# A gap of 64 bytes in SBUF: weights and the tiles they are multiplied with, moved apart modulo 128 bytes

## The chip, the core and the metric

The kernel runs on one core of one Trainium2 chip. A core has five engines that run side by side: TensorE (PE in the profile; its weight loads are shown apart as PEld), VectorE (DVE), ScalarE (ACT), GpSimd (POOL) and SyncE (SP, which here only issues DMAs). They work on tiles in SBUF, a memory of 128 partitions. A tile has the same byte offset in every partition, and this offset is what the change is about. TensorE writes its results to eight banks in PSUM.

The metric is the device time of one execution in microseconds (us). Three runs of the kernel before gave 505.38, 505.47 and 506.69 us, median 505.47 us.

## What is computed

One decoder block over 512 tokens of 1,024 channels, in float32: a norm, one wide projection, sparse attention (mixer A), chunked retention (mixer B), a gated merge, an output projection, a second norm and the residual. Cut to the lines that make the matrix products:

```python
h = rms_norm(x, norm_pre)
proj = h @ w_in
...
o_a = jax.vmap(nsa_fn)(q_n, k_c, v_c, k_s, v_s, k_w, v_w, gate_n)
y_a = (o_a * jax.nn.silu(z_n)) @ w_nsa_o
...
o_b = jax.vmap(retention_sequence)(q_r, k_r, v_r)
y_b = (o_b * jax.nn.silu(z_r)) @ w_ret_o
merged = jax.nn.sigmoid(m_a) * y_a + jax.nn.sigmoid(m_b) * y_b
x = x + rms_norm(merged @ w_out, norm_post)
```

## The kernel before

**Products in three parts.** A float32 operand is split in a high part, rounded to the type fp32r, and a low part, the rest. A product a*b is then three matmuls of fp32r that add up in one PSUM bank: high*high, low*high and high*low (`mm3`, and the same three by hand in `tra`, `seven`, `pair` and `out_seven`). In the profile the parts are named apart: `hTh` and `hTl` are the high and low parts of the transposed h, `whi` and `wlo` those of a piece of weights.

**Two ways round.** A matmul row reads `bank<-moving,stationary`: the second tile is loaded into the array (the LDWEIGHTS rows of PEld), the first one is streamed through it. `nat` streams weights against a stationary piece of h (`bank<-whi,hTh`, 512 columns). `tra` keeps a piece of weights stationary and streams h (`bank<-hTh,whi`, 512 columns). In `seven`, four quarters of a weight block and sums of them are multiplied 256 columns at a time with quarters of h (`bank<-hTh,whi`, 256 columns) and with sums of quarters of h, which lie in other tiles, named `shorts` (`bank<-shorts,whi`, 256 columns). Attention and retention multiply tiles of one large tile, `arena_r`, with each other (`bank<-arena_r`). Transpositions (L263) stream an identity matrix, `identr`, against a stationary `shorts` tile. Nearly all matmuls are issued by the helper at L257; L1234 and L1725 are the blocks `pair` and `out_seven`.

**Weights.** A stream of weights comes from DRAM by DMA into four `raw` tiles. ScalarE (L224, sometimes VectorE, L232) writes the high part to one of nine `whi` tiles, VectorE (L236) the low part to one of nine `wlo` tiles. GpSimd queues DMAs that add blocks of weights in DRAM (`pair`, `t`, `out`).

**Order.** The order of all instructions is fixed when the program is built, by a planner with costs for each engine; each engine runs its own list and waits on semaphores. The planner's costs know shapes, not addresses.

**Where tiles lie.** Pools take SBUF from low to high in the order in which they are opened: first a block `room` of 58 KB, over which tiles named `words` and `shorts` are laid, then the pools `small`, `const`, `wts` (9 `whi` and 9 `wlo`, 2,048 bytes each), `hT`, `big` (`arena_r` and `rsrow`) and `raw`. The places follow from this and from the sizes of the tiles:

| tiles | first byte, before | modulo 128, before |
|---|---|---|
| `room` (`words`, `shorts`) | 2,176 | 0 |
| `identr` | 63,104 | 0 |
| `kc`, `vcs` (compressed keys and values) | 67,488 and 68,000 | 32 |
| `whi`, `wlo` | 69,056 | 64 |
| `hTh`, `hTl` | 105,920 and 122,304 | 64 |
| `arena_r` | 138,688 | 64 |
| `raw` | 212,416 | 64 |

Almost every tile cut from these starts a multiple of 128 bytes further on, so that it keeps its class modulo 128. The exception is the second block of weights, pieces of 280 columns (1,120 bytes) in `arena_r`, whose classes go round 64, 32, 0, 96.

Of the kernel before, what the change touches and what calls it, by code (L numbers as in the profile page):

```python
# [10 lines left out]
FT = mybir.dt.float32  # L11
# [7 lines left out]
P = 128  # L19
# [131 lines left out]
def block_kernel(ctx: ExitStack, tc, x, xT, x0s, ws, small, w2s, norm_post, rope_r, dmask, out):  # L151
# [22 lines left out]
    hp_ = ctx.enter_context(tc.tile_pool(name="hT", bufs=1))  # L174
# [109 lines left out]
    nhalf = cp.tile([P, 4], FT, name="nhalf")  # L284
    G.memset(nhalf, -0.5)

    hTh = hp_.tile([P, KD, SEQ], FR, name="hTh")
    hTl = hp_.tile([P, KD, SEQ], FR, name="hTl")

# [1696 lines left out]
```

## Time and profile before

| | us |
|---|---|
| median of three runs | 505.47 |
| the profiled execution, whole | 504.99 |
| its span, first to last instruction | 503.2 |
| PE busy / PEld / DVE / ACT / POOL | 493.7 / 421.4 / 424.6 / 324.7 / 39.3 |

The profile comes from one execution. The span is what its rows add up to; 1.8 us lie around it. In a row such as `x48 | 13.6, 282` stand the number of instructions, the time in which at least one of them ran, and the mean length of one in ns. A matmul's length is longer than its share of the engine, since the next one starts before it ends: how fast TensorE goes is read from the starts of successive rows, or from a number of matmuls in a stretch without idle time.

### The profile page before, as it was taken

How to read it: one execution, taken by the hardware profiler on the slowest of the kernel's cores; microseconds unless marked ns; L12 is line 12 of the kernel's file. 1: busy time of each engine (PE TensorE's matmuls, PEld its weight loads, DVE VectorE, ACT ScalarE, POOL GpSimd, SP SyncE). 2: the span in 40 equal slices, each digit the busy share in tenths (PEclk: the TensorE clock that was granted, in tenths of full speed). 3: DMA queues.
4: the chain of work that ended last, by engine and by line, in shares of the span. 5: the costliest groups of instructions: out<-in, count | busy, mean ns of one | idle time of the engine just before them, and what ended most of it. 6: DMA issues, size and time to landing. Idle time of an engine off the chain costs nothing.

```text
span 503.2 us, 7872 instructions
## 1 busy us (share of the span) xinstructions
PE 493.7 (98%) x2666; PEld 421.4 (84%) x2666; DVE 424.6 (84%) x996; ACT 324.7 (65%) x722; POOL 39.3 (8%) x66
## 2 busy tenths in 40 slices
PE   8999999999999999999999999999999999999994
PEld 7898887888888888888888888888888989988883
DVE  6698899989989989998789999778787867979795
ACT  6795599558679788784587574835435535527642
POOL 3102100023000210000100000101000000000010
PEclk9999999999999999999999999999999999999999
DMA  8968995779998899325556673530473735635813
GB/s 318 385 211 283 326 227 200 242 136 225 370 238 182 262 293 211 113 85 166 119 173 212 215 235 114 126 126 8 162 250 113 233 116 191 199 113 169 303 56 142
DMA packets 31080, 98.75 MB, mean 196 GB/s; under 512 B 3136, under 2 KB 6976, under 8 KB 30272
## 3 DMA queue, kind: packets, MB, share of 16 engines
q1 hardware_dynamic: 24576, 70.85, 41.5%
q0 software_dynamic: 6320, 27.26, 22.9%
q8 instruction: 21, 0.34, 0.3%
q14 instruction: 19, 0.16, 0.1%
q10 hardware_dynamic: 144, 0.14, 0.1%
HBM read 93.52 MB, written 31.98 MB: 249 GB/s over the span
## 4 chain that ended last, share of the span: by engine, by line
PE 89%; DMA 5%; DVE 4%; issue 1%; ACT 0%; POOLq 0%; DVEq 0%; POOL 0%; ACTq 0%; SPq 0%
PE bank L257 70%; PE bank L1234 8%; PE bank L1725 7%; PE bank L263 4%; DMA raw<-in_stream_dram 3%; DVE arena_r L236 1%; DMA words<-in_xT_dram 1%; DVE wlo L236 1%; DMA words<-in_x_dram 1%; DVE words L236 1%; DVE words L679 0%; DVE words L249 0%; DVE words L243 0%; DVE words L967 0%; DVE whi L232 0%
## 5 line engine op out<-in xcount | busy, mean ns | idle before, releaser
L224 ACT ACTIVATE whi<-raw 128x512 fp32r<-128x512 f32 x177 | 107.0, 627 | 53.4 <-PE bank L257 36.2
L236 DVE TENSOR_TENSOR wlo<-raw,whi 128x512 fp32r<-128x512 f32 x188 | 123.4, 685 | 10.4 <-ACT whi L224 9.5
L257 PE MATMUL bank<-whi,hTh 128*128 128x512 f32 x192 | 74.0, 407 | 0.3 <-ACT hTh L224 0.3
L257 PE MATMUL bank<-arena_r 128*128 128x256 f32 (+2 forms) x328 | 70.7, 335 | 0.7 <-DVE arena_r L236 0.5
L257 PE MATMUL bank<-whi,hTl 128*128 128x512 f32 x192 | 71.2, 391 | 0.0
L257 PE MATMUL bank<-wlo,hTh 128*128 128x512 f32 x192 | 71.0, 390 | 0.0
L224 ACT ACTIVATE arena_r<-bank 128x512 fp32r<-128x512 f32 (+3 forms) x104 | 49.1, 476 | 26.3 <-PE bank L263 25.4
L236 DVE TENSOR_TENSOR arena_r<-bank,arena_r 128x512 fp32r<-128x512 f32 (+3 forms) x104 | 56.0, 542 | 9.6 <-ACT arena_r L224 8.5
L257 PE MATMUL bank<-arena_r,whi 128*128 128x512 f32 (+1 forms) x208 | 63.6, 381 | 0.0
L224 ACT ACTIVATE words<-words,stat 128x128 f32<-128x128 f32 (+3 forms) x105 | 54.1, 546 | 6.6 <-DVE stat L967 4.9
L257 PEld LDWEIGHTS bank<-arena_r 128*128 128x128 f32 x328 | 50.8, 189 | 7.6 <-DVE arena_r L236 1.2
L257 PE MATMUL bank<-hTh,whi 128*128 128x512 f32 (+1 forms) x144 | 52.2, 363 | 0.0
L257 PE MATMUL bank<-hTh,wlo 128*128 128x512 f32 (+1 forms) x144 | 51.4, 357 | 0.0
L257 PE MATMUL bank<-hTl,whi 128*128 128x512 f32 (+1 forms) x144 | 51.1, 355 | 0.0
L257 PEld LDWEIGHTS bank<-arena_r,whi 128*128 128x128 f32 x208 | 38.8, 188 | 7.3
L257 PEld LDWEIGHTS bank<-whi,hTl 128*128 128x128 f32 x192 | 36.2, 188 | 8.0
L257 PEld LDWEIGHTS bank<-whi,hTh 128*128 128x128 f32 x192 | 36.5, 191 | 6.9 <-ACT hTh L224 0.6
L257 PEld LDWEIGHTS bank<-wlo,hTh 128*128 128x128 f32 x192 | 36.1, 188 | 6.3
L257 PE MATMUL bank<-arena_r,wlo 128*128 128x512 f32 x96 | 37.3, 389 | 0.0
L263 PEld LDWEIGHTS bank<-identr,shorts 128*128 128x128 f32 x268 | 30.1, 140 | 8.6 <-DVE arena_r L236 0.9
L224 ACT ACTIVATE words<-words 128x512 f32<-128x512 f32 (+3 forms) x47 | 27.2, 586 | 12.8 <-DVE words L236 8.0
L263 PE MATMUL bank<-identr,shorts 128*128 128x128 f32 x268 | 31.6, 238 | 0.5 <-DVE arena_r L236 0.5
(182 smaller groups left out, 891.0 us busy)
## 6 DMA issues: line engine op xcount, KB each, us to landing
raw<-in_stream_dram SPq DMA_DIRECT2D x73, 512.0 KB, 4.4
pair<-in_stream_dram POOLq DMA_DIRECT2D x6, 1024.0 KB, 11.8
t<-in_stream_dram POOLq DMA_DIRECT2D x6, 1024.0 KB, 17.2
out<-in_stream_dram POOLq DMA_DIRECT2D x6, 1024.0 KB, 17.1
words<-in_x_dram SPq DMA_DIRECT2D x8, 512.0 KB, 6.9
raw<-s SPq DMA_DIRECT2D x8, 512.0 KB, 4.2
raw<-pair SPq DMA_DIRECT2D x8, 512.0 KB, 4.2
raw<-t SPq DMA_DIRECT2D x8, 512.0 KB, 3.6
```

The lines of the kernel that those rows point to most:

```text
L224: S.activation(o, i, func, **kw)
L236: (V if e == "dve" else G).tensor_tensor(o, a, b, op=op)
L257: T.matmul(ps, a, b, start=start, stop=stop)
L263: T.transpose(ps, a, idn)
L1234: T.matmul(ps[m], a, b, start=n in first and s + j == 0, stop=n in last and s + j == 5, skip_group_check=True)
L1725: T.matmul(ps[m], a, b, start=n in first and s + i == 0, stop=n in last and s + i == 5, skip_group_check=True)
```

## The change

One tile of 16 float32 (64 bytes in each partition) is taken from the pool `hT` ahead of `hTh` and is never used:

```diff
     nhalf = cp.tile([P, 4], FT, name="nhalf")
     G.memset(nhalf, -0.5)

+    hp_.tile([P, 16], FT, name="room16")
     hTh = hp_.tile([P, KD, SEQ], FR, name="hTh")
     hTl = hp_.tile([P, KD, SEQ], FR, name="hTl")
```

Every tile from `hTh` on moves up by 64 bytes; `room`, `identr`, `kc`, `vcs`, `whi` and `wlo` stay where they are. Each engine has the same instructions in the same order as before, PE 2,653 matmuls among them; only addresses differ.

| a matmul's moving and stationary tile | modulo 128, before | after |
|---|---|---|
| weights with `hTh`, `hTl` or `arena_r`, either way round | 64 and 64 | 64 and 0, or 0 and 64 |
| `arena_r` with `arena_r` or `hTh` | the same class (or 280-column pieces, all four differences) | the same differences |
| `shorts` with weights | 0 and 64 | 0 and 64 |
| `identr` with `shorts` | 0 and 0 | 0 and 0 |
| VectorE's low part: `raw`, `whi` read, `wlo` written | 64, 64, 64 | 0, 64, 64 |

The four `raw` tiles, 192 past a multiple of 256 bytes before, come to multiples of 256.

## The prediction

> **What bounds the kernel now.** I read the page first, then the windows, then the chain of waits.
>
> ```profile
> span 503.2 us, 7872 instructions
> ...
> PE 493.7 (98%) x2666; PEld 421.4 (84%) x2666; DVE 424.6 (84%) x996; ACT 324.7 (65%) x722; POOL 39.3 (8%) x66
> ...
> PE 89%; DMA 5%; DVE 4%; issue 1%; ACT 0%; POOLq 0%; DVEq 0%; POOL 0%; ACTq 0%; SPq 0%
> ```
>
> TensorE is busy 493.7 of 503.2 us and is 89% of the chain that ended last. The windows (PE, PEld, DVE, ACT, POOL busy with counts, granted clock, DMA share, GB/s) show where that is strict:
>
> ```profile
> 34.00:100.00 66.00, 64.58 (x378) 54.78 (x377) 60.64 (x159) 50.27 (x116) 6.34 (x10) 1.00 0.81 251
> 100.00:250.00 150.00, 150.00 (x804) 125.98 (x804) 133.15 (x373) 110.39 (x291) 18.11 (x22) 1.00 0.77 199
> 250.00:355.00 105.00, 105.00 (x543) 88.93 (x542) 91.41 (x197) 69.17 (x135) 6.37 (x8) 1.00 0.50 154
> 355.00:495.00 140.00, 140.00 (x782) 122.65 (x782) 110.42 (x196) 68.42 (x128) 1.69 (x2) 1.00 0.52 173
> ```
>
> From 100 to 495 us TensorE has no idle time at all, at a granted clock of 1.00. A nanosecond less per matmul is there a nanosecond less in the end, as long as VectorE, at 133 of 150 us the next, keeps up. So the question is only the step from one matmul to the next. The chain, in order of time (start, length, what), gives the step of the wide ones:
>
> ```profile
> 354.67 103.93 PE bank L257 x621
> 458.59 35.37 PE bank L1725 x156
> ```
>
> The 156 matmuls of 512 columns at L1725 take 35.37 us: 226.7 ns each, with both tiles 64 past a multiple of 128. Now the narrow ones, 256 columns, in `seven` (timeline: start, length):
>
> ```profile
> 391.10 0.28 PE L257 MATMUL bank<-hTh,wlo 128*128 128x256 f32 x1
> ...
> 392.18 0.28 PE L257 MATMUL bank<-hTh,wlo 128*128 128x256 f32 x1
> ...
> 392.66 0.39 PE L257 MATMUL bank<-shorts,whi 128*128 128x256 f32 x2
> ...
> 393.68 0.39 PE L257 MATMUL bank<-shorts,whi 128*128 128x256 f32 x2
> ```
>
> From the first to the second row nine matmuls start in 1.08 us, 120 ns each; from the third to the fourth nine in 1.02 us, 113.3 ns each. Shape, stationary weights, loop and clock are the same. What differs is where the moving tile lies: `hTh` at 64, in the class of the weights, `shorts` at 0, in the other. And 113.3 is exactly half of 226.7: both are the step in which the columns alone set the pace, and `hTh` pays 6.7 ns on top. I read this as two streams of one engine, the moving columns and the next weight load, that get in each other's way when they lie in the same half of 128 bytes; that a 512-column matmul pays nothing in a steady run means that its longer step hides the collision. After the change every such pair of weights with `hTh`, `hTl` or `arena_r` stands as `shorts` with weights stands now.
>
> **The change, term by term.** No instruction is added, removed or moved on any queue, and no wait. Only steps can change.
>
> Narrow matmuls with h moving and weights stationary, and the same with `shorts`, grouped by form:
>
> ```profile
> L257 PE MATMUL bank<-shorts,whi 128*128 128x256 f32 x112 | 21.0, 277 | 0.0
> L257 PE MATMUL bank<-shorts,wlo 128*128 128x256 f32 x64 | 17.7, 277 | 0.0
> L257 PE MATMUL bank<-hTh,wlo 128*128 128x256 f32 x48 | 13.6, 283 | 0.0
> L257 PE MATMUL bank<-hTl,whi 128*128 128x256 f32 x48 | 13.6, 282 | 0.0
> L257 PE MATMUL bank<-hTh,whi 128*128 128x256 f32 x48 | 13.6, 282 | 0.0
> L257 PE MATMUL bank<-arena_r,whi 128*128 128x256 f32 x16 | 4.5, 281 | 0.0
> ```
>
> 3 x 48 + 16 = 160 matmuls change class, all between 385 and 437 us, where nothing but TensorE decides: 160 x 6.7 ns = **1.07 us less**. The bounds are nothing (the class isn't the cause) and the same 1.07 us.
>
> Wide matmuls in the mixed stages. The lengths of one, from the forms between 40 and 350 us, and two rows from 350 to 497 us:
>
> ```profile
> L257 PE MATMUL bank<-whi,hTh 128*128 128x512 f32 x160 | 64.5, 403 | 0.0
> L257 PE MATMUL bank<-whi,hTl 128*128 128x512 f32 x160 | 62.6, 391 | 0.0
> L257 PE MATMUL bank<-wlo,hTh 128*128 128x512 f32 x160 | 62.5, 390 | 0.0
> L257 PE MATMUL bank<-hTh,whi 128*128 128x512 f32 x91 | 36.7, 404 | 0.0
> L257 PE MATMUL bank<-hTh,wlo 128*128 128x512 f32 x91 | 35.8, 394 | 0.0
> L257 PE MATMUL bank<-hTl,whi 128*128 128x512 f32 x91 | 35.6, 391 | 0.0
> ...
> L257 PE MATMUL bank<-arena_r,whi 128*128 128x512 f32 x192 | 59.2, 389 | 0.0
> L257 PE MATMUL bank<-arena_r,wlo 128*128 128x512 f32 x96 | 37.3, 389 | 0.0
> ```
>
> In the steady stage one lasts 389 ns. In the mixed stages the four kinds that don't come first behind a transposition last 1 to 5 ns more, and the step is longer by as much, as the timeline shows:
>
> ```profile
> 166.04 0.46 PE L257 MATMUL bank<-whi,hTh 128*128 128x512 f32 x1
> 166.34 0.39 PE L257 MATMUL bank<-wlo,hTh 128*128 128x512 f32 x1
> ...
> 168.43 0.39 PE L257 MATMUL bank<-whi,hTl 128*128 128x512 f32 x1
> ```
>
> From 166.34 to 168.43 nine wide matmuls start, 232 ns each in place of 226.7: a matmul that has been put off by short ones before it makes up for it only over many steps, as one would expect where a wide one has no slack. The sum over the four rows is 160 x 2 + 160 x 1 + 91 x 5 + 91 x 2 = 1,117 ns for 502 matmuls, 2.2 ns each; the same 2.2 ns for the 251 of the two first kinds (whose means of 403 and 404 hold a pause of some 75 ns behind a transposition, 166.04 to 166.34, that is no matter of addresses) make 0.56 us more. Bounds: nothing, and 1.7 us. With the other class there is slack to catch up, but the short matmuls before (arena with arena, transpositions) still collide, since their classes don't change. I take half: **0.85 us less**.
>
> Narrow matmuls of the hidden layer (`bank<-whi,arena_r`, about 75 to 97 us) change class too, but there TensorE waits for the low part:
>
> ```profile
> 76.16 0.38 PE L257 MATMUL bank<-wlo,arena_r 128*128 128x256 f32 x1 [0.47 <-DVE wlo L236]
> ...
> L263 PE MATMUL bank<-identr,shorts 128*128 128x128 f32 x268 | 31.6, 238 | 0.5 <-DVE arena_r L236 0.5
> ```
>
> 64 of them x 6.7 ns would be 0.43 us; what hides it is that wait, which grows by what the matmuls save. I count nothing.
>
> Pairs that get worse: the 268 transpositions stand in some 67 groups of four. Behind a group, `identr` moves at 0 while a piece of h or arena is loaded, at 64 before and at 0 after; ahead of it, an h or arena tile moves at 0 while `shorts` is loaded. At most 67 x 2 x 6.7 ns = 0.9 us more; the pause of 75 ns behind each group and the wide matmul ahead of it should cover most. I take **0.15 us more**, bounds 0 and 0.9.
>
> VectorE and ScalarE read `raw` at 0 in place of 64. VectorE's subtraction with tiles at 0 and 64 read and 64 written is there already, from `words`:
>
> ```profile
> L236 DVE TENSOR_TENSOR wlo<-raw,whi 128x512 fp32r<-128x512 f32 x188 | 123.4, 685 | 10.4 <-ACT whi L224 9.5 <-PE bank L257 0.4
> L236 DVE TENSOR_TENSOR arena_r<-words,arena_r 128x512 fp32r<-128x512 f32 x15 | 10.1, 682 | 0.0
> ```
>
> 682 against 685 ns: 3 ns x 188 = 0.6 us of VectorE at most, off the chain. Nothing. DMAs into `raw` are on the chain only in the first 26 us, in two pieces:
>
> ```profile
> 9.66 7.84 DMA raw<-in_stream_dram
> ...
> 18.77 6.68 DMA raw<-in_stream_dram
> ```
>
> [...]
>
> **Sum.** 1.07 + 0.85 - 0.15 = 1.77 us less: 504.99 becomes 503.22 us. The profiled execution is 0.48 us below the median of the runs, so a median of **503.7 us**.
>
> **Rivals.**
>
> *Nothing happens.* What sets `shorts` apart may be another thing than bit 6 of the address: `shorts` lie in the first 62 KB, all else behind. For it: only one pair of tiles shows the gain. Against it: weights with h and arena with weights lie in quite different places and all stand at 120 or 226.7. Time 505.4. [...]
>
> *Only the narrow ones gain.* The wide ones' 2.2 ns come from something else in the mixed stages, and the loss at the transpositions is somewhat larger: between 0.5 and 1.5 us less, at the middle 504.5.
>
> *Slower: the wide ones lose.* If the collision hangs on where in the step the weight load reads, the wide ones may be free of it now because of the equal class, and pay with unequal ones. For it: the one place where a wide matmul at 64 is followed by a load from 0 is the one ahead of a transposition, and it is slow:
>
> ```profile
> 208.82 0.40 PE L257 MATMUL bank<-whi,hTl 128*128 128x512 f32 x1
> 209.06 0.45 PE L263 MATMUL bank<-identr,shorts 128*128 128x128 f32 x4
> ```
>
> 0.24 us in place of 0.227. Against it: a transposition is another kind of load, and narrow ones are free with unequal classes. Price 6.7 ns for each of the 753 + 288 wide matmuls of the rows above, 7.0 us, less the 1.07 of the narrow ones: 505.5 + 5.9 = 511.4. It decides as soon as more than 1.77 us / 6.7 ns = 264 wide matmuls pay.
>
> **Chances and range.** The forecast, with all between 1.5 and 3.2 us less (1.07 + 1.7 + 0.43): 0.52. Only the narrow ones: 0.19. Nothing, within 0.5 us: 0.21. Slower: 0.08. A measurement of this kernel tells about 0.3%, 1.5 us, from no change. Faster by more than that: 0.52; within: 0.40; slower: 0.08. The range goes from 505.5 - 3.2 = 502.3 to 505.8, nothing gained and a third of the 0.9 us lost at transpositions; the slower rival is left out.
>
> **What would show it.** Right: narrow `hTh,whi` at 113 ns a step and a length of 277; the four wide kinds at 389 to 390 in the mixed stages; 156 matmuls at L1725 in 35.4 us as before. Wrong: `hTh,whi` still at 120 (then it is not the class), L1725 at 36.4 us (then wide ones pay), or new waits of TensorE for `wlo` between 100 and 250 us (then VectorE takes the gain).

## The result, and the profile after

| | median, us | lowest to highest | profiled execution, us | its span, us |
|---|---|---|---|---|
| before | 505.50 | 505.38 to 506.69 (4 runs) | 504.99 | 503.2 |
| after | 509.91 | 509.25 to 510.25 (4 runs) | 509.25 | 507.5 |

The ratio is 1.008, with a 95% interval from 1.0061 to 1.010: the kernel is 4.4 us slower, where 1.8 us less was forecast. The page of the kernel after (span, busy time of the engines, shares of the chain that ended last):

```profile
span 507.5 us, 7872 instructions
...
PE 498.2 (98%) x2666; PEld 421.2 (83%) x2666; DVE 424.8 (84%) x996; ACT 325.2 (64%) x722; POOL 39.2 (8%) x66
...
PE 95%; DVE 2%; issue 1%; DMA 1%; ACT 0%; POOLq 0%; POOL 0%; DVEq 0%; ACTq 0%
```

TensorE is busy for 4.5 us more (498.2 against 493.7) with the same number of instructions (2,666 matmul rows in both pages; the 2,653 given with the change stands in neither), VectorE and ScalarE for 0.2 and 0.5 us more. So no wait has come in: the same matmuls take longer. TensorE's share of the chain, 95% against 89%, is no part of the loss: before, the chain ran over DMAs up to 25.45 us, here it runs over TensorE from 4.65 us on, and the 121st matmul starts 28.7 us into the span before and 28.8 after. The windows (busy time with counts of PE, PEld, DVE, ACT, POOL, then granted clock, DMA share, GB/s) say the same by stage:

```profile
34.00:100.00 66.00, 64.56 (x378) 54.74 (x377) 60.99 (x161) 50.73 (x116) 6.30 (x10) 1.00 0.82 251
100.00:250.00 150.00, 150.00 (x795) 124.75 (x795) 131.60 (x367) 109.99 (x289) 18.11 (x22) 1.00 0.76 198
250.00:355.00 105.00, 105.00 (x535) 87.65 (x535) 89.97 (x196) 67.17 (x131) 6.37 (x8) 1.00 0.49 149
355.00:495.00 140.00, 140.00 (x777) 121.53 (x777) 110.27 (x194) 68.82 (x127) 1.69 (x2) 1.00 0.51 170
```

From 100 to 495 us TensorE still has no idle time and the granted clock is still 1.00, but in the same three stretches it gets 9, 8 and 5 matmuls less done (804, 543 and 782 before). The end of the chain, in order of time (start, length, what):

```profile
357.35 104.67 PE bank L257 x621
462.03 36.20 PE bank L1726 x156
```

(Lines behind the new one are numbered one higher: L1726 is L1725 of before.) Against the rows of before, 354.67 with 103.93 and 458.59 with 35.37, the stages up to the last transposition bring 357.35 - 354.67 = 2.68 us, the 621 matmuls behind it 0.74 us, the last 156 another 0.83 us: together 4.25 of the span's 4.3. These 156 wide matmuls go at 36.20 / 156 = 232.1 ns a step in place of 226.7. Lengths, by form, between 40 and 350 us:

```profile
L257 PE MATMUL bank<-whi,hTl 128*128 128x512 f32 x160 | 63.2, 395 | 0.0
L257 PE MATMUL bank<-wlo,hTh 128*128 128x512 f32 x160 | 63.1, 394 | 0.0
...
L257 PE MATMUL bank<-hTl,whi 128*128 128x512 f32 x88 | 34.6, 394 | 0.0
L257 PE MATMUL bank<-hTh,wlo 128*128 128x512 f32 x88 | 34.6, 393 | 0.0
```

and between 350 and 501 us:

```profile
L257 PE MATMUL bank<-arena_r,whi 128*128 128x512 f32 x192 | 59.6, 392 | 0.0
...
L257 PE MATMUL bank<-shorts,wlo 128*128 128x256 f32 x64 | 18.0, 281 | 0.0
L257 PE MATMUL bank<-hTh,wlo 128*128 128x256 f32 x48 | 13.4, 278 | 0.0
...
L1726 PE MATMUL bank<-whi,arena_r 128*128 128x512 f32 x32 | 10.1, 396 | 0.0
```

Apart from those that come first behind a transposition, wide matmuls with weights moving are longer in every row, 394 to 396 ns (389 to 391 before); those with weights stationary last 392 to 394 (389 to 394 before), longer in all rows but `hTh` over `wlo`, 393 against 394. Narrow ones with h fell from 283 to 278, near the 277 of the forecast, but those with `shorts`, which like the weights did not move at all, rose from 277 to 281. From the starts of successive rows, summed over the whole trace (what a start comes later than 226.7 or 113.3 ns behind the one before, longer pauses left out): wide with weights moving 0.94 to 5.24 us, wide with weights stationary 0.62 to 1.56, narrow with h 1.01 to 0.52, narrow with `shorts` 0.16 to 0.77. Those four bring 5.4 us; all other steps, the longer pauses of TensorE among them, give 1.1 back.

### The profile page after: what moved, and what is told of

Same layout as the page of the kernel before. It is cut to its first block, busy times and chain, and to the rows that moved or that the text cites. A ratio compares the mean times of both kernels' runs of the same rounds, so it can differ in the third digit from the quotient of the medians.

```text
span 507.5 us, 7872 instructions
## 1 busy us (share of the span) xinstructions
PE 498.2 (98%) x2666; PEld 421.2 (83%) x2666; DVE 424.8 (84%) x996; ACT 325.2 (64%) x722; POOL 39.2 (8%) x66
## 4 chain that ended last, share of the span: by engine, by line
PE 95%; DVE 2%; issue 1%; DMA 1%; ACT 0%; POOLq 0%; POOL 0%; DVEq 0%; ACTq 0%
PE bank L257 76%; PE bank L1235 8%; PE bank L1726 7%; PE bank L263 4%; DVE arena_r L236 1%; DMA words<-in_x_dram 1%; DVE wlo L236 1%; DVE words L249 0%; DVE words L236 0%; DVE words L968 0%; DVE words L243 0%; ACT words L224 0%; POOLq L1983 0%; POOL rr L236 0%; DVEq L1983 0%
```

## The experiments

The theories that the expectations name by letters: **A**, the prediction's own rule turned round, only bit 6 of the difference counts and unequal halves cost the wide matmuls time; **B**, h and `arena_r` at multiples of 128 are bad in themselves; **C**, it is `raw` at multiples of 128 or 256; **D**, any move costs, by higher bits of the address; **E**, what counts is the stationary tile's address less the moving one's, modulo 256 or 512, and 0 is the one place that is free for wide matmuls; **F**, the two places don't matter, another engine's traffic does; **G**, narrow matmuls have two lasting states, and what runs ahead of them decides which. In E, weights moving over h (`nat`) and h moving over weights (`tra`) have opposite differences: with a gap of 64, `nat` stands at 64 and `tra` at 192. The diffs are against the kernel after; ratios are against runs of the kernel before on the same chip, whose medians were 505.53 (e1 to e4), 505.73 (e5 to e8) and 505.13 (e9 to e11).

**A gap of 128.** Weights, h and `arena_r` are all 64 past a multiple of 128 again, at a difference of 128.

```diff
-    hp_.tile([P, 16], FT, name="room16")
+    hp_.tile([P, 32], FT, name="room16")
```

> The gap is 128 bytes in place of 64: h, arena and raw are back at 64 past a multiple of 128, at other addresses than before. Theory A (a matmul's step depends on the difference modulo 128 bytes between its moving tile and the stationary tile loaded beside it; wide matmuls, 512 columns, pay for unequal halves of 128): 505.5 us, the 156 matmuls at the out block in 35.4 us. Theory B (h and arena at multiples of 128 are bad in themselves): 505.5 us. Theory C (raw at multiples of 128 or 256 is bad for those who read or write it): 505.5 us. Theory D (any move of these tiles makes it slower, by bits above the seventh): 509.9 us.

510.77 us, ratio 1.0099 (1.0083 to 1.0116): not back at 505.5, but slower than with 64. By form, 350 to 505 us:

```profile
L257 PE MATMUL bank<-arena_r,whi 128*128 128x512 f32 x192 | 60.3, 395 | 0.0
```

395 ns in place of 389, though the two tiles have the same class modulo 128. A falls: bit 6 is not what sets the wide step. B and C forecast 505.5 too; only D, at 509.9, had a loss here.

**All of them moved.** The 64 bytes stand ahead of the weights, so that weights, h, `arena_r` and `raw` all come to multiples of 128 and stay where they were against each other.

```diff
-    hp_.tile([P, 16], FT, name="room16")
+    wp.tile([P, 16], FT, name="room16")
```

> The 64 bytes lie ahead of the weights, so weights, h, arena and raw all come to multiples of 128. Theory A: wide matmuls as before, 226.7 ns a step; the 176 narrow ones with shorts moving now stand in one half with the weights and go from 113 to 120 ns, 1.2 us more: 506.7 us. Theory B: 509.9 us. Theory C: 509.9 us.

505.77 us, ratio 1.0002 (0.9990 to 1.0014). By form, 350 to 501 us:

```profile
L257 PE MATMUL bank<-arena_r,whi 128*128 128x512 f32 x192 | 59.2, 390 | 0.0
...
L257 PE MATMUL bank<-shorts,wlo 128*128 128x256 f32 x64 | 18.0, 282 | 0.0
```

h, `arena_r` and `raw` lie at multiples of 128 and nothing is lost: B falls, and with it the thought that the loss has to do with where one tile lies. `shorts`, which now has a difference of 128 to the weights, went from 277 to 282.

**Only `raw`.**

```diff
-    hp_.tile([P, 16], FT, name="room16")
+    rp.tile([P, 16], FT, name="room16")
```

> Only the raw tiles move by 64 bytes. Theories A and B: 505.5 us, every matmul step as before. Theory C: 509.9 us, with longer ScalarE and VectorE rows on raw, or longer DMAs.

504.84 us, ratio 0.9985 (0.9972 to 0.9998): within 0.3% of before. C falls.

**Only `arena_r` (and `raw`), h not.**

```diff
+    bp.tile([P, 16], FT, name="room16")
     arena_r = bp.tile([P, 70 * 256], FR, name="arena_r")
...
-    hp_.tile([P, 16], FT, name="room16")
```

> The 64 bytes lie between h and arena: h stays at 64 with the weights, arena (and raw) come to 0. Theory A: steps with weights moving and h stationary stay at 226.7 ns, those with weights moving and arena stationary go to 233 ns (178 of them, 1.2 us), those with arena moving and weights stationary to 229 ns (300 of them, 0.6 us): 507.3 us. Theory B: about a third of the loss, since arena alone is at a multiple of 128, with the arena-by-arena steps longer too: 507 us, told from A by arena-by-arena steps. Theory C: 509.9 us.

506.84 us, ratio 1.0026 (1.0015 to 1.0038). By form, 350 to 501 us:

```profile
L258 PE MATMUL bank<-arena_r,whi 128*128 128x512 f32 x192 | 59.5, 391 | 0.0
...
L258 PE MATMUL bank<-shorts,wlo 128*128 128x256 f32 x64 | 17.7, 277 | 0.0
...
L1726 PE MATMUL bank<-whi,arena_r 128*128 128x512 f32 x32 | 10.0, 395 | 0.0
L1726 PE MATMUL bank<-whi,hTl 128*128 128x512 f32 x24 | 9.3, 389 | 0.0
```

In one and the same block, L1726, the matmuls over `arena_r` cost 395 ns and those over `hTl` 389. It follows the pair, not the block or another engine. `shorts` with weights stays at the 277 of before.

**Steps by themselves.** A kernel that leaves the whole computation out: 40 matmuls in a row, the moving tile fixed, the stationary one 0, 32, 64 up to 480 bytes past a multiple of 512, first with 512 columns, then with 256.

```python
for n in (512, 256):
    for _, s in sta:
        ...
        for i in range(STEPS):
            T.matmul(b[:, 0:n], s[:, i % 4 * P:(i % 4 + 1) * P], mov[:, 0:n], start=i == 0, stop=i == STEPS - 1)
```

> Not the block but a rig: it leaves the whole computation out and streams one moving tile against stationary tiles that lie 0, 32, 64 ... 480 bytes further on modulo 512, 40 matmuls each, first 512 columns wide, then 256; a matmul that waits for VectorE stands between two sections. Theory E (the step depends on the difference of the two places modulo 256 or 512, and 0 is the one place where a wide matmul pays nothing): wide 226.7 ns at 0 (and at 256, if the period is 256), 229 to 233 ns at all others; narrow 120 ns at 0 and 113 to 120 at others. Theory A (only the half of 128 bytes counts, modulo 128): the same step at 0, 128, 256 and 384. Theory F (it is not the two places but something else in the block, such as other engines' accesses): 226.7 and one and the same narrow step at all sixteen places.

Its chain of waits has one row for each section (start, length, what). The first ten are those at 0, 32, 64, 96, 128, 160, 192, 224, 256 and 288:

```profile
14.42 9.08 PE bank L50 x40
...
24.46 9.40 PE bank L50 x40
...
34.81 9.40 PE bank L50 x40
...
45.17 9.44 PE bank L50 x40
...
55.57 9.36 PE bank L50 x40
...
65.89 9.39 PE bank L50 x40
...
76.24 9.24 PE bank L50 x40
...
86.44 9.39 PE bank L50 x40
...
96.79 9.14 PE bank L50 x40
...
106.89 9.40 PE bank L50 x40
```

All but the first begin behind a pause, so that 9.14, at 256, is what they are to be held against: (9.40 - 9.14) / 39 = 6.7 ns more a step at 32 and 64, (9.36 - 9.14) / 39 = 5.6 at 128, (9.24 - 9.14) / 39 = 2.6 at 192. Read from the starts in the steady part, a wide step is 226.7 ns at 0, 233.3 at 32, 64, 160 and 224, 234.3 at 96, 232.1 at 128 and 228.9 at 192; from 256 on the same values come again. F falls: no other engine works during a section. Only 0 modulo 256 is free. Narrow ones, by form:

```profile
L50 PE MATMUL bank<-mov,at0b 128*128 128x256 f32 x40 | 5.0, 284 | 0.0
...
L50 PE MATMUL bank<-mov,at64b 128*128 128x256 f32 x40 | 4.9, 282 | 0.0
...
L50 PE MATMUL bank<-mov,at320b 128*128 128x256 f32 x40 | 4.8, 278 | 0.0
```

Here 0 is one of the slowest places, at 120.0 ns a step, and 160 is no faster (120.1). The others have between 116.7 and 118.7, but for 320, which has 113.3 where 64 has 117.8. That was not expected: the same difference modulo 256, and two lasting steps.

**A gap of 256.**

```diff
-    hp_.tile([P, 16], FT, name="room16")
+    hp_.tile([P, 64], FT, name="room16")
```

> The gap is 256 bytes. Theory E with a period of 256: 505.5 us, wide steps 226.7 ns. Theory E with a period of 512: slower, 509 to 511 us, wide steps up to 233 ns. Theory A with its period of 128 has fallen with the gap of 128 bytes.

505.26 us, ratio 0.9990 (0.9980 to 1.0000): as before. For the wide matmuls the period is 256, and D falls.

**A gap of 32.**

```diff
-    hp_.tile([P, 16], FT, name="room16")
+    hp_.tile([P, 8], FT, name="room16")
```

> The gap is 32 bytes, half of the change. Theory E: slower, 507 to 511 us, since any difference but 0 costs; if the cost grows with the distance, about half of the change's 4.4 us: 507.7 us.

511.67 us, ratio 1.0118 (1.0102 to 1.0135), the slowest of all and above the 507 to 511 that E gave: the cost does not grow with the distance. Both ways round stand at 233.3 in the steps by themselves.

**A gap of 512.**

```diff
-    hp_.tile([P, 16], FT, name="room16")
+    hp_.tile([P, 128], FT, name="room16")
```

> The gap is 512 bytes, the length of one stationary piece in a partition. Theory E with a period of 256 or 512: 505.5 us. If it is the distance itself that counts and no period: 510 us.

505.10 us, ratio 0.9992 (0.9982 to 1.0001): as before.

**A gap of 192.** `nat` and `tra` change roles: `nat` at 192, `tra` at 64.

```diff
-    hp_.tile([P, 16], FT, name="room16")
+    hp_.tile([P, 48], FT, name="room16")
```

> The gap is 192 bytes: h and arena are at multiples of 128 as in the change, 64 below the weights modulo 256 where the change has them 64 above. Theory E with the rig's steps (the place of the stationary tile less that of the moving one, modulo 256: 0 gives 226.7 ns, 64 gives 233.3, 192 gives 228.9): the two ways round change roles, 836 wide steps with weights moving pay 2.2 ns, 546 with weights stationary pay 6.7 ns, 5.5 us in place of the change's 836 x 6.7 + 546 x 2.2 = 6.8 us; the change cost 4.4 us, 0.65 of that, so here 3.6 us: 509.1 us. By form: h moving and weights stationary go to the longer length, weights moving to the shorter. Theory B (h and arena at multiples of 128): the same as the change, 509.9 us, and the same lengths.

508.52 us, ratio 1.0068 (1.0052 to 1.0085). By form, 350 to 501 us:

```profile
L257 PE MATMUL bank<-arena_r,whi 128*128 128x512 f32 x192 | 60.4, 396 | 0.0
...
L257 PE MATMUL bank<-hTh,wlo 128*128 128x256 f32 x48 | 13.2, 276 | 0.0
...
L1726 PE MATMUL bank<-whi,hTl 128*128 128x512 f32 x24 | 9.4, 392 | 0.0
```

With 64 it was the other way round, 392 for `arena_r` over `whi` and 396 for `whi` over `arena_r`. The sign of the difference counts, as E has it. Narrow matmuls with h, here at a difference of 64, last 276 ns (283 before), and their row starts come 113.4 ns apart: in this run they have nearly the whole gain that the prediction forecast for the change, and the wide ones take it away.

**Only h.**

```diff
+    bp.tile([P, 48], FT, name="room48")
     arena_r = bp.tile([P, 70 * 256], FR, name="arena_r")
...
     hp_.tile([P, 16], FT, name="room16")
```

> 64 bytes ahead of h and 192 more ahead of arena: h alone is displaced against the weights, arena is back at a difference of 0 modulo 256. Theory E: the other part of the change, 658 wide steps with weights moving and h stationary x 6.7 ns and 248 with h moving x 2.2 ns, 4.9 us by the rig, 0.65 of it 3.2 us: 508.7 us; with the gap between h and arena (1.3 us) it adds up to the change's 4.4 us. Steps with arena and weights at 226.7 ns. If the parts don't add up, the loss has to do with something all tiles share, and theory E is at most half of it.

508.70 us, ratio 1.0073 (1.0058 to 1.0088). By form, 350 to 501 us:

```profile
L258 PE MATMUL bank<-shorts,wlo 128*128 128x256 f32 x64 | 18.0, 281 | 0.0
...
L1727 PE MATMUL bank<-whi,arena_r 128*128 128x512 f32 x32 | 9.9, 389 | 0.0
L1727 PE MATMUL bank<-whi,hTl 128*128 128x512 f32 x24 | 9.5, 396 | 0.0
```

The mirror of the run with `arena_r` alone: now `hTl` pays and `arena_r` doesn't. `shorts` with weights, neither of which moved, goes to 281 here and stayed at 277 there: it loses where h, multiplied just ahead of it in `seven`, has moved. By medians, h alone costs 3.6 us and `arena_r` alone 1.3; together 4.9, against 4.4 for the change, which moves both.

**Both addresses, and what runs ahead.** A second kernel that leaves the whole computation out: four places of the moving tile by four of the stationary one; one section whose stationary tile alternates between 0 and 64; and narrow sections at differences of 64 and 192 behind six matmuls of different kinds (`lead`).

```python
for m in ms:
    for s in sta:
        section(none, m, [s], 512)
section(none, ms[0], [sta[0], sta[1]], 512)
for lead in (none, (ms[0], sta[0], 512, 6), (ms[0], sta[1], 512, 6), (ms[0], sta[2], 512, 6), (ms[0], sta[3], 512, 6),
             (ms[0], sta[0], 256, 6), (ms[0], sta[0], 128, 6), (ms[0], sta[0], 64, 6)):
    for s in (sta[1], sta[3]):
        section(lead, ms[0], [s], 256)
```

> A second rig, again without the block's computation. First four places of the moving tile (0, 64, 128, 192 modulo 256) against four places of the stationary tiles, wide: theory E says that only the difference counts, 226.7, 233.3, 232.1 and 228.9 ns for 0, 64, 128 and 192 whatever the moving tile's own place; theory B says that the moving or the stationary place alone shifts the step. Then stationary tiles that alternate between 0 and 64: steps of 226.7 and 233.3 in turn, or 230 at the mean. Then narrow sections at a difference of 64 and of 192, each behind another lead (a pause, six wide matmuls at 0, 64, 128, 192, six narrow ones, six of 128 and of 64 columns): theory G (at one and the same difference the narrow step has two lasting states, 113.3 and 117.8 ns, and what runs ahead decides) says that both steps turn up; if the difference alone decided, all eight leads would give one step each.

Its chain: moving and stationary tile at 0 and 64, 64 and 64, 64 and 128, 128 and 192, 192 and 0, then the alternating section, then narrow ones at 64 and 192 behind a pause, and at 64 and 192 behind six narrow ones at 0 (counted in):

```profile
23.43 9.40 PE bank L44 x40
...
64.48 9.16 PE bank L44 x40
...
74.60 9.40 PE bank L44 x40
...
125.91 9.39 PE bank L44 x40
...
136.27 9.39 PE bank L44 x40
...
177.24 9.37 PE bank L44 x40
...
187.56 4.62 PE bank L44 x40
...
193.14 4.77 PE bank L44 x40
...
255.03 5.49 PE bank L44 x46
261.48 5.31 PE bank L44 x46
```

The four pairs that differ by 64 have 9.39 to 9.40 wherever they lie, the equal one 9.16: only the difference counts. Of the sixteen pairs fifteen came as expected; at a difference of 128 one (moving 64, stationary 192) went at 233.3 in place of 232.1, perhaps a second state there too. The alternating section missed its expectation: 232.5 ns a step rather than the 230 halfway between the two. A load from 0 doesn't come free between loads from 64. G holds in this run: at 64 a narrow step is 113.3 ns behind a pause or wide ones, 117.8 behind six narrow ones at 0; at 192 it is 117.8 behind a pause, 113.3 behind those six. The addresses are the same each time, so here what runs ahead decides. It does not account for the first kernel of steps, where 64 went at 117.8 and 320 at 113.3, both behind a pause. Worked out from the sizes of the tiles, the difference modulo 512 is 64 there and 320 here, so that behind a pause the narrow step may go by 512 bytes; that was not tested.

## Why the prediction was wrong

**What bounds the kernel: right.** From 100 to 495 us TensorE is never idle, in either kernel. A nanosecond per matmul came out in the end, only with the other sign: 4.5 us more of PE busy, 4.3 us more of span.

**The step that failed** is the reading of the 120 and 113.3 ns as "two streams of one engine ... that get in each other's way when they lie in the same half of 128 bytes", with its second half, "that a 512-column matmul pays nothing in a steady run means that its longer step hides the collision". Everything else was built on "After the change every such pair of weights with `hTh`, `hTl` or `arena_r` stands as `shorts` with weights stands now". That the step hangs on the two addresses was right: in the steps by themselves, with nothing else running, a wide one takes 226.7 ns at a difference of 0 and 233.3 at 64. By what means the difference slows the step, no run shows. The rule was drawn from one narrow pair, and the wide ones were taken to be free at any place because they were free at the only place at which the kernel before has them, a difference of 0. That place is the one exception for wide matmuls (226.7 ns, up to 234.3 elsewhere), and one of the slowest for narrow ones (120.0). Nor is it halves of 128 bytes: at a gap of 128 the classes are equal and the time was 510.77. The remark that the narrow step with `shorts` is exactly half of the wide one, 113.3 against 226.7 ns, showed that 0 is free for wide ones, not that all places are.

**Narrow ones, 1.07 us less: right in sign, half in size.** Row starts give 0.49 us less for h with weights. In the first `seven` after, `hTh,whi` goes at 118 ns, in the second at 113.3 (timeline: start, length):

```profile
389.54 0.28 PE L257 MATMUL bank<-hTh,whi 128*128 128x256 f32 x1
...
394.49 0.28 PE L257 MATMUL bank<-hTh,whi 128*128 128x256 f32 x1
...
420.31 0.28 PE L257 MATMUL bank<-hTh,whi 128*128 128x256 f32 x1
...
425.07 0.28 PE L257 MATMUL bank<-hTh,whi 128*128 128x256 f32 x1
```

Between the first two rows 42 matmuls start in 4.95 us, 117.9 each; between the last two 42 in 4.76, 113.3 each: the two states that the second kernel of steps shows. They also fit how `shorts`, at 64 from the weights before and after, could lose 0.61 us without having moved: the matmuls ahead of it did, and it lost in the run that moved h alone (281) and not in the one that moved `arena_r` alone (277).

**Wide ones in the mixed stages, 0.85 us less: wrong.** The prediction was right that behind short matmuls the wide ones go slower for many steps (before, nine of 232 ns from 166.34 us on), but the slack was to come from the change. It took the free place away. Weights moving over h or `arena_r` came to 64, at 6.7 ns a step in the steps by themselves; weights stationary came to 192, at 2.2. By 836 steps with weights moving and 546 with weights stationary, the counts in the expectation for the gap of 192 (the kernel has 864 and 576 such matmuls in all), that is 836 x 6.7 + 546 x 2.2 = 6.8 us as an upper sum; measured are 4.4. The same sum for the gap of 192, with the roles changed, is 5.5 against 3.4 measured, for 32 it is 9.2 against 5.9, for 128 7.5 against 5.2. The order of the variants comes out right, the size at about two thirds. The row starts show for the change where the missing third is. After it, wide starts come 5.24 + 1.56 = 6.8 us late, just the sum; but 0.94 + 0.62 = 1.56 us of it stood there before, so that only 5.24 is new. The narrow ones add 0.12 on balance, and all other steps give 1.1 back, which leaves the span's 4.3. So for wide steps with h the new step took the place of what they already lost before, 1.5 ns a step with weights moving and 2.9 with h moving; it did not come on top. Why the other steps shrink by 1.1 us stays open.

**Transpositions, `raw`, VectorE: nothing seen.** VectorE's busy time rose by 0.2 us, and `raw` alone at multiples of 256 measured within 0.3% of before. A gain from `raw` can't be told from none: with `raw` alone at multiples of 256 the median is 504.84 (504.43 to 506.21) against 505.53, 0.69 less, but the gap of 512, which leaves `raw` at 192, is 0.63 less, and the run with all tiles moved, which has `raw` at multiples of 256, 0.24 more.

**The rivals.** *Slower: the wide ones lose* is what happened, at 509.9 against the 511.4 that it gave, in the way that it named, wide ones free at an equal place and paying at unequal ones (226.7 ns a step at a difference of 0, 233.3 at 64), though equal means modulo 256, not 128. Its one row, the 0.24 us of a wide matmul ahead of a load from another place, pointed the right way, but not all of it need be the address: the 24 steps from weights moving to a load of `shorts` in the trace of before have a median of 233 ns, where the difference between these tiles, 192, gave 228.9 in the steps by themselves. It was priced at one value for all 1,041 matmuls; there are two, by the sign of the difference. Its sign, L1726 at 36.4 us, came as 36.20. It got 0.08 because "narrow ones are free with unequal classes" was held against it, the step that fell. *Nothing happens* was 505.4, and fell: with nothing but matmuls running, a wide step goes from 226.7 to 233.3 ns by address alone. *Only the narrow ones gain* fell with the wide rows.

No version beat both kernels by more than a measurement tells: gaps of 256 and 512 and `raw` alone lie within 0.3% of before. Narrow pairs at 64 with wide ones still at 0 would need other places for the pieces of weights in `seven`, for about 1 us at most (the 1.01 us of the row starts, which the gap of 192 did gain on its narrow ones); it wasn't tried.

## What to carry to other kernels

Where TensorE is never idle, look at the step between starts, for each pair of tiles, against the shortest that the same number of columns shows (here 226.7 ns for 512 and 113.3 for 256), and keep the stationary tile's address less the moving one's at a multiple of 256 bytes for matmuls of 512 columns (226.7 ns there, 228.9 to 234.3 elsewhere; fp32r, 128 x 128 weights; nothing else was tried); a few bytes in one pool shift every pool behind it. A form that shows no cost at the one place where a kernel has it is not shown to be free at others: before building on such a row, ask whether the trace holds the form at a second place. A short kernel that steps through the places by itself costs one run and would have told the sign here.

## What the runs showed of the hardware that was not expected

- In the two kernels of steps the step of fp32r matmuls of 512 columns in a row depended on the stationary address less the moving one, modulo 256 bytes: 226.7 ns at 0 and 228.9 (192) to 234.3 ns (96) elsewhere. Both addresses moved together changed nothing: the four pairs that differ by 64 took 9.39 to 9.40 us for 40, and the run with all tiles moved 505.77 us against 505.53.
- For 256 columns 0 and 160 were the slowest places in the first of them, 120.0 and 120.1 ns; elsewhere the step was 113.3 to 118.7.
- For 256 columns there were two lasting steps between the same two tiles in the second, 113.3 and 117.8 ns at differences of 64 and of 192, kept for a whole section of 40; with the addresses the same, six matmuls of another kind ahead were enough to change from one to the other. A pair of tiles lost time when another was moved: `shorts` with weights went from 277 to 281 ns when h alone moved.
